# Newton steps of the norm with an operand in PSUM, and a softmax that starts its row minimum at the sink, in an encoder trunk on Trainium2

## The chip, the cores and the metric

The kernel runs on one core of one Trainium2 chip. The metric is the device time of one execution in microseconds (us); a version is described by the median of several executions. A core has five engines that run their own instruction streams and wait for each other by semaphores: TensorE (PE, the matrix engine, whose results land in the PSUM memory), VectorE (DVE), ScalarE (ACT), GpSimd (POOL), and SyncE (SP), which here issues nearly all DMAs. All other data of the kernel lie in the on-chip memory SBUF.

## The reference

Two token sequences, a prompt of 512 tokens and a sample of 1024, go through two layers with the same weights (model width 1024). What matters of one layer:

```python
hn = rmsnorm(h, ln1[i])                      # h * rsqrt(mean(h*h) + EPS) * gain
q, k, v, ga, uf, gf, mga, mgf = split(hn @ w_in[i])
a = band_attention(rope(q), rope(k), v, sink[i]) * silu(ga)
f = fourier_mix(uf, w_fmix[i]) * silu(gf)
h = h + (sigmoid(mga) * (a @ w_ao[i]) + sigmoid(mgf) * (f @ w_fo[i])) @ w_out[i]
h = h + (p[i] @ w_pe[i]) * sigmoid(rmsnorm(h, ln_pg[i]) @ w_pg[i])
```

and, inside the attention (8 query heads, 2 key heads, head width 64, a band of 128 tokens to each side, one sink number `sk` per head):

```python
m = maximum(max(s, axis=-1), sk)             # s = q k^T / 8, masked by -1e30
e = exp(s - m)
pr = e / (sum(e, axis=-1) + exp(sk - m))
```

A last rmsnorm gives the output.

## The kernel before

**Tiling.** Tokens are cut into three chunks of 512 columns: chunk 0 is the prompt, chunks 1 and 2 (called the pair) are the sample. Features lie on the 128 partitions, so that h of one chunk is 8 tiles of 128x512. All products are fp32 emulated by three matmuls: `hi_lo` splits an operand into a rounded high part (an ACT cast, L86) and the rest (a subtraction on DVE or POOL, L87), and `mm3` issues high by high, high by low and low by high (L98, L99, L100).

**Stages of a layer.** `project_prompt` computes the 34 column tiles of the input projection of the prompt, with three other streams woven in by `run`: making the normed pair, the prompt's attention, and the prompt's Fourier branch. `project_pair` does the projection of both sample chunks by a scheme with seven half products (L231 the matmuls, L238 to L260 the sums of them), with the pair's attention woven in. Then `merge` of the prompt, with the sample's Fourier branch beside it, and `merge` of the pair follow: branch projections, output projection, a norm, the gate projection, the residual update. The kernel is traced under a scheduler that takes the program order as priorities and sets each engine's final order from its own model of times and from free buffers. A different list of instructions in one place can so come out in another order on every engine nearby.

**The norm.** `Norm.add` sums squares of the 8 tiles. `Norm.stats` (L302 to L315) contracts them over partitions by four matmuls with a column of 1/1024 (L305) into columns 0 to 3 of a PSUM bank of the tag misc, 128 tokens on the partitions and 4 groups of tokens in the columns. L307 adds EPS, giving `v`; L309 and L310 make the first guess of 1/sqrt(v) by integer operations on the bits; three Newton steps of three operations each follow (L312 a product r * -0.5 * r, L313 a product with v, L314 the new r). All these are 128x4 operations on DVE; all but L307 read and write small SBUF tiles of the tag tiny. `Norm.scale` (L317 to L323) then turns r into a row form by four PE transposes into another misc bank (L320), and a DVE copy brings that to SBUF (L322). There are 15 such norms in a run. PE takes its instructions in order, so while L320 waits for the last L314, every matmul behind L320 waits too.

**The softmax.** A unit is 128 queries with one key head, thus 4 query heads; there are 8 units for the prompt and 16 for the sample per layer, 48 in all, with 192 heads. A unit's window W is 384 keys, at the two ends of a sequence 256. `scores(u)` (L658 to L689) does per head: two matmuls into a PSUM bank sc (L670, 2 banks), a custom DVE reduction (L675) that adds the mask, writes the masked scores to SBUF and the row maximum to `mx`, a DVE operation that makes the bias min(-0.125 mx, -sink) (L678), and the exponential on ACT with its row sum (L680). Then, once per unit, a DVE addition (L683), an exponential of the sink terms on ACT (L684), a DVE addition to the sum (L685), a DVE reciprocal (L686), and four ACT operations that scale the probabilities (L688). `values(u)` (L691 on) transposes the probabilities on PE (L707) into misc banks, splits them (L86 on ACT, L87 on DVE), and multiplies them with the values (L712) into the bank o. In the prompt, the program gives `scores(u)` ahead of `values(u-1)`; in the pair, `scores(u)` and `values(u)` follow each other with four slots of the projection between.

**Who else uses DVE and POOL.** The subtractions L87 go to DVE for activations and partly to POOL, above all for weights (386 of 128x512 from act tiles, and 72 from scr tiles, on POOL). The activation functions of the projection are finished on DVE (L427) after an ACT tanh (L426).

Of the kernel before, what the change touches and what calls it, by code (L numbers as in the profile page):

```python
# [18 lines left out]
P = 128  # L19
# [20 lines left out]
def trunk(ctx: ExitStack, tc: tile.TileContext, x, p, w_in, w_af, w_out, w_pe, w_pg, w_fm,  # L40
# [20 lines left out]
    def big(shape, dt=F32):  # L61
        return sbt(shape, dt, "act")
# [226 lines left out]
    class Norm:  # L289
# [12 lines left out]
        def stats(self):  # L302
            st = pst("misc")
            for j in range(4):
                PE.matmul(st[:, j : j + 1], self.acc[:, j * P : (j + 1) * P], mean_sb, start=True, stop=True)  # L305
            v, r, z = (sbt([P, 4], F32, "tiny") for _ in range(3))
            V.tensor_scalar(v, st[:, 0:4], EPS, None, op0=ALU.add)  # L307

            V.tensor_scalar(r.bitcast(I32), v.bitcast(I32), 1, None, op0=ALU.arith_shift_right)  # L309
            V.tensor_scalar(r.bitcast(I32), r.bitcast(I32), -1.0, float(0x5F3759DF), op0=ALU.mult, op1=ALU.add)  # L310
            for _ in range(3):
                V.scalar_tensor_tensor(z, r, -0.5, r, op0=ALU.mult, op1=ALU.mult)  # L312
                V.tensor_tensor(z, z, v, op=ALU.mult)  # L313
                V.scalar_tensor_tensor(r, z, 1.5, r, op0=ALU.add, op1=ALU.mult)  # L314
            self.r = r  # L315
# [316 lines left out]
    def attention(l, chunks, slim):  # L632
# [25 lines left out]
        def scores(u):  # L658
# [5 lines left out]
            mx, nmx, rs, es, rd = (sbt([P, 4], F32, "stat") for _ in range(5))  # L664
            probs = []
            for i in range(4):
# [4 lines left out]
                if i % 2 == 0:  # L671
                    t = big([P, 2, W])
                pr, e = t[:, i % 2, :], slice(i, i + 1)
                probs.append(pr)
                V.tensor_tensor_reduce(out=pr, in0=sc[:, :W], in1=msk, scale=1.0, scalar=-3.0e38,  # L675
                                       op0=ALU.add, op1=ALU.max, accum_out=mx[:, e])

                V.scalar_tensor_tensor(nmx[:, e], mx[:, e], -0.125, nsink_sb[:, l, head : head + 1],  # L678
                                       op0=ALU.mult, op1=ALU.min)
                S.activation(pr, pr, AF.Exp, bias=nmx[:, e], scale=0.125, accum_out=rs[:, e])  # L680
                if i % 2:
                    yield
            V.tensor_tensor(es, sink_sb[:, l, 4 * kv : 4 * kv + 4], nmx, op=ALU.add)  # L683
            S.activation(es, es, AF.Exp)  # L684
            V.tensor_tensor(rd, rs, es, op=ALU.add)  # L685
            V.reciprocal(rd, rd)  # L686
            for i, pr in enumerate(probs):
                S.activation(pr, pr, AF.Copy, scale=rd[:, i : i + 1])  # L688
# [419 lines left out]
```

## Time and profile before

| what | value |
|---|---|
| time, median of 3 runs | 2336.91 us (2334.51 to 2337.52) |
| profiled execution, its own time | 2336.8 us |
| its span in the trace | 2334.6 us |
| PE busy | 2211.7 us, 95% |
| DVE busy | 1424.6 us, 61% |
| POOL busy | 1113.4 us, 48% |
| ACT busy | 1088.9 us, 47% |
| mean granted TensorE clock | 0.98 |

The profile is of one execution. In its views, a row of the timeline gives the start and the duration in us, the engine, the source line, the operation, the tiles (out<-in), the shape, and how many instructions the row holds; in brackets stands how long the engine sat idle before it and what it waited for. A row of the groups gives after the bar the busy time in us and the mean duration in ns, and after the second bar the idle time before these instructions and what ended it. The view of one line gives min, median and max duration in ns, the first and last start, and the shapes. The view of waits gives, for PE, how long each line waited for which other line, in all, how many times, and the longest. A view of windows gives for stretches of time how long each engine was busy, with the number of instructions, and the granted clock of PE.

### The profile page before, as it was taken

The numbers are of one execution on the slowest core, as the hardware profiler recorded it, in microseconds if no ns is written. First come the engines' busy times: TensorE is split into PE (matmuls) and PEld (weight loads), VectorE is DVE, ScalarE is ACT, GpSimd is POOL, SyncE is SP. The second block draws the span as 40 slices with busy tenths as digits, with TensorE's granted clock in tenths as the row PEclk, the third lists the DMA queues.
The fourth block names the chain that finished last, engine by engine and source line by source line (L and its number), as shares of the span: only waits on it lengthen the run. The fifth ranks groups of instructions, "written<-read, shape, count | busy, mean of one in ns | idle before, by whom it ended". The sixth has DMA issues, their size and how long they took to land. (4 is left out here: it accounts for less than half of the span.)

```text
span 2334.6 us, 30544 instructions
## 1 busy us (share of the span) xinstructions
PE 2211.7 (95%) x10176; PEld 1812.2 (78%) x10176; DVE 1424.6 (61%) x2563; ACT 1088.9 (47%) x2292; POOL 1113.4 (48%) x827
## 2 busy tenths in 40 slices
PE   8899999999998989999999999899999999999986
PEld 6677777888877877888887787788787788788875
DVE  5866645677566775252767653657766666744376
ACT  5467433466664444223424853336666544422331
POOL 1313446444446863344514355644444568554471
PEclk9899999999999999999999999999999999999998
DMA  7565435445437464731445554453444655553232
GB/s 280 187 198 177 164 119 178 147 140 165 131 130 269 153 237 163 249 117 47 140 166 185 153 177 168 149 171 125 148 154 132 218 198 186 198 194 117 87 113 95
DMA packets 240542, 380.73 MB, mean 163 GB/s; under 512 B 21121, under 2 KB 95489, under 8 KB 240385
## 3 DMA queue, kind: packets, MB, share of 16 engines
q1 hardware_dynamic: 233472, 366.19, 46.6%
q10 hardware_dynamic: 6912, 12.59, 1.5%
q8 instruction: 81, 1.33, 0.2%
q14 instruction: 77, 0.62, 0.1%
HBM read 270.17 MB, written 108.53 MB: 162 GB/s over the span
## 5 line engine op out<-in xcount | busy, mean ns | idle before, releaser
L87 POOL TENSOR_TENSOR act<-act,act 128x512 fp32r<-128x512 f32 x386 | 547.2, 1437 | 463.4 <-ACT act L86 403.8
L231 PE MATMUL mm<-act,act 128*128 128x512 f32 x2856 | 700.4, 395 | 27.6 <-DVE act L87 11.7
L231 PEld LDWEIGHTS mm<-act,act 128*128 128x128 f32 x2856 | 531.1, 189 | 147.2 <-ACT act L86 18.0
L98 PE MATMUL mm<-act,act 128*128 128x512 f32 x1408 | 563.1, 400 | 29.6 <-ACT act L86 28.5
L100 PE MATMUL mm<-act,act 128*128 128x512 f32 x1408 | 559.3, 399 | 13.2 <-POOL act L87 13.2
L99 PE MATMUL mm<-act,act 128*128 128x512 f32 x1408 | 557.8, 396 | 0.0
L86 ACT CAST act<-act 128x512 fp32r<-128x512 f32 x574 | 330.1, 619 | 223.0 <-DMA act<-in_w_af 53.2
L98 PEld LDWEIGHTS mm<-act,act 128*128 128x128 f32 x1408 | 269.8, 192 | 88.6 <-ACT act L86 35.0
L100 PEld LDWEIGHTS mm<-act,act 128*128 128x128 f32 x1408 | 269.3, 191 | 78.2 <-POOL act L87 23.4
L99 PEld LDWEIGHTS mm<-act,act 128*128 128x128 f32 x1408 | 269.7, 192 | 54.0
L87 DVE TENSOR_TENSOR act<-scr,act 128x512 fp32r<-128x512 f32 x188 | 180.7, 979 | 102.8 <-ACT act L86 101.6
L86 ACT CAST act<-scr 128x512 fp32r<-128x512 f32 (+1 forms) x260 | 152.6, 614 | 170.8 <-DVE scr L382 79.0
L87 POOL TENSOR_TENSOR act<-scr,act 128x512 fp32r<-128x512 f32 (+1 forms) x72 | 100.1, 1392 | 207.6 <-ACT act L86 141.1
L87 DVE TENSOR_TENSOR act<-act,act 128x512 fp32r<-128x512 f32 x188 | 172.2, 944 | 35.7 <-ACT act L86 34.7
L300 POOL TENSOR_TENSOR scr<-scr,scr 128x512 f32<-128x512 f32 x67 | 94.5, 1411 | 173.5 <-ACT scr L299 164.1
L299 ACT ACTIVATE scr<-act 128x512 f32<-128x512 f32 x105 | 65.3, 632 | 236.8 <-DVE act L540 148.1
L680 ACT ACTIVATE act<-act,stat 128x384 f32<-128x384 f32 (+1 forms) x192 | 111.0, 580 | 68.9 <-DVE stat L678 68.5
L87 DVE TENSOR_TENSOR act<-misc,act 128x512 fp32r<-128x512 f32 x132 | 88.5, 687 | 76.8 <-ACT act L86 76.3
L86 ACT CAST act<-misc 128x512 fp32r<-128x512 f32 x132 | 73.7, 586 | 96.1 <-PE misc L707 93.6
L675 DVE CUSTOM_DVE_ANT_0 act<-sc,mask_sb 128x384 f32<-128x384 f32 (+1 forms) x192 | 92.4, 508 | 41.8 <-PE sc L670 36.7
L100 PE MATMUL sc<-act,act 128*128 128x512 f32 (+1 forms) x292 | 111.8, 383 | 1.1 <-DVE act L87 1.1
L98 PE MATMUL sc<-act,act 128*128 128x512 f32 (+1 forms) x292 | 111.5, 383 | 0.0
(209 smaller groups left out, 3019.3 us busy)
## 6 DMA issues: line engine op xcount, KB each, us to landing
act<-in_w_in SPq DMA_DIRECT2D x136, 256.0 KB, 4.3
act<-in_w_in SPq DMA_DIRECT2D x68, 512.0 KB, 4.7
gt<-scr SPq DMA_DIRECT2D x96, 256.0 KB, 2.3
scr<-gt SPq DMA_DIRECT2D x96, 256.0 KB, 5.3
act<-in_w_pg SPq DMA_DIRECT2D x80, 256.0 KB, 3.7
act<-in_w_af SPq DMA_DIRECT2D x64, 256.0 KB, 4.8
act<-in_w_out SPq DMA_DIRECT2D x64, 256.0 KB, 4.9
pl<-scr ACTq DMA_DIRECT2D x48, 256.0 KB, 2.5
```

The source lines that it names most:

```text
L86: S.copy(hi, src)
L87: lo_eng.tensor_tensor(lo, src, f(hi), op=ALU.subtract)
L98: PE.matmul(out, wh, xh, start=i == 0, stop=False)
L99: PE.matmul(out, wh, xl, start=False, stop=False)
L100: PE.matmul(out, wl, xh, start=False, stop=i == n - 1)
L231: PE.matmul(bank, w, v, start=first and k == 0 and n == 0, stop=k == 3 and n == 2, skip_group_check=True)
L299: S.activation(sq, h, AF.Square)
L300: eng.tensor_tensor(self.acc, self.acc, sq, op=ALU.add)
L675: V.tensor_tensor_reduce(out=pr, in0=sc[:, :W], in1=msk, scale=1.0, scalar=-3.0e38, op0=ALU.add, op1=ALU.max, accum_out=mx[:, e])
L680: S.activation(pr, pr, AF.Exp, bias=nmx[:, e], scale=0.125, accum_out=rs[:, e])
```

## The change

In `Norm.stats`, v, y (the shifted bits) and z get columns 4 to 15 of the PSUM bank that holds the sums, in place of SBUF tiles; r stays in an SBUF tile of the tag tiny. The first two operations of a Newton step change places: z = v * r, then z = z * -0.5 * r. There are 12 DVE operations as before; each now has one operand in PSUM and at most one tensor in SBUF. The misc bank of the sums is held until the last Newton step, where it was free after L307 before.

In `scores`, the reduction scales by -0.125 and takes the minimum, and begins at the negated sink (a per-partition scalar read through a pointer to SBUF, where it was the constant -3e38), so that it yields the bias itself. L678 is gone. The masked scores are now scaled when they are written, and the exponential has scale -1. The tile of two heads has one more column, into which a new ACT copy of 128x2 (L676 of the changed kernel, one per two heads) writes the negated sink; the exponential runs over W+1 columns, so its row sum includes the sink's term, and L683, L684 and L685 are gone. The reciprocal takes the row sum directly, and the normalisation runs over W columns. Per unit, 6 DVE operations and one on ACT go, and two on ACT come.

In the changed kernel the lines stand a little lower: L320 becomes L322, L670 becomes L672, L675 becomes L680, L680 becomes L683, L427 becomes L429; the reciprocal stays L686 and the normalisation L688.

```diff
@@ -303,14 +303,16 @@
             st = pst("misc")
             for j in range(4):
                 PE.matmul(st[:, j : j + 1], self.acc[:, j * P : (j + 1) * P], mean_sb, start=True, stop=True)
-            v, r, z = (sbt([P, 4], F32, "tiny") for _ in range(3))
+
+            v, y, z = (st[:, 4 * j : 4 * j + 4] for j in range(1, 4))
+            r = sbt([P, 4], F32, "tiny")
             V.tensor_scalar(v, st[:, 0:4], EPS, None, op0=ALU.add)
 
-            V.tensor_scalar(r.bitcast(I32), v.bitcast(I32), 1, None, op0=ALU.arith_shift_right)
-            V.tensor_scalar(r.bitcast(I32), r.bitcast(I32), -1.0, float(0x5F3759DF), op0=ALU.mult, op1=ALU.add)
+            V.tensor_scalar(y.bitcast(I32), v.bitcast(I32), 1, None, op0=ALU.arith_shift_right)
+            V.tensor_scalar(r.bitcast(I32), y.bitcast(I32), -1.0, float(0x5F3759DF), op0=ALU.mult, op1=ALU.add)
             for _ in range(3):
-                V.scalar_tensor_tensor(z, r, -0.5, r, op0=ALU.mult, op1=ALU.mult)
-                V.tensor_tensor(z, z, v, op=ALU.mult)
+                V.tensor_tensor(z, v, r, op=ALU.mult)
+                V.scalar_tensor_tensor(z, z, -0.5, r, op0=ALU.mult, op1=ALU.mult)
                 V.scalar_tensor_tensor(r, z, 1.5, r, op0=ALU.add, op1=ALU.mult)
             self.r = r
 
@@ -661,7 +663,7 @@
             W = (k1 - k0) * P
             msk = mask_sb[:, (k0 - qb + 1) * P : (k1 - qb + 1) * P]
             q, kw = blocks[c, b][kv]["q"], blocks[c, b][kv]["kw"]
-            mx, nmx, rs, es, rd = (sbt([P, 4], F32, "stat") for _ in range(5))
+            nmx, rs, rd = (sbt([P, 4], F32, "stat") for _ in range(3))
             probs = []
             for i in range(4):
                 head = 4 * kv + i
@@ -669,23 +671,21 @@
                 for j in range(2):
                     PE.matmul(sc[:, :W], q[:, i, :], kw[:, j, :], start=j == 0, stop=j == 1)
                 if i % 2 == 0:
-                    t = big([P, 2, W])
+
+                    t = big([P, 2, W + 1])
+                    S.copy(t[:, :, W], nsink_sb[:, l, head : head + 2])
                 pr, e = t[:, i % 2, :], slice(i, i + 1)
                 probs.append(pr)
-                V.tensor_tensor_reduce(out=pr, in0=sc[:, :W], in1=msk, scale=1.0, scalar=-3.0e38,
-                                       op0=ALU.add, op1=ALU.max, accum_out=mx[:, e])
-
-                V.scalar_tensor_tensor(nmx[:, e], mx[:, e], -0.125, nsink_sb[:, l, head : head + 1],
-                                       op0=ALU.mult, op1=ALU.min)
-                S.activation(pr, pr, AF.Exp, bias=nmx[:, e], scale=0.125, accum_out=rs[:, e])
+
+                V.tensor_tensor_reduce(out=pr[:, :W], in0=sc[:, :W], in1=msk, scale=-0.125,
+                                       scalar=nsink_sb[:, l, head : head + 1],
+                                       op0=ALU.add, op1=ALU.min, accum_out=nmx[:, e])
+                S.activation(pr, pr, AF.Exp, bias=nmx[:, e], scale=-1.0, accum_out=rs[:, e])
                 if i % 2:
                     yield
-            V.tensor_tensor(es, sink_sb[:, l, 4 * kv : 4 * kv + 4], nmx, op=ALU.add)
-            S.activation(es, es, AF.Exp)
-            V.tensor_tensor(rd, rs, es, op=ALU.add)
-            V.reciprocal(rd, rd)
+            V.reciprocal(rd, rs)
             for i, pr in enumerate(probs):
-                S.activation(pr, pr, AF.Copy, scale=rd[:, i : i + 1])
+                S.activation(pr[:, :W], pr[:, :W], AF.Copy, scale=rd[:, i : i + 1])
             blocks[c, b][kv]["probs"] = probs
 
         def values(u):
```

The order of the instructions also changes, in the attention stages only; the rows that follow were printed without times. In the prompt of the first layer, PE reaches its first scores as follows in the kernel before (L98 to L100 are projection matmuls, `sc` the score banks, `misc` the banks of the transposes, and the numbers behind the names count tiles):

```order
L670 MATMUL sc_1167<-act_1125,scr_1123 128x256 x2
L670 MATMUL sc_1174<-act_1125,scr_1123 128x256 x2
L98 MATMUL mm_1287<-act_346,act_1154 128x512
L99 MATMUL mm_1287<-act_346,act_1154 128x512
L670 MATMUL sc_1199<-act_1131,scr_1129 128x256 x2
L670 MATMUL sc_1206<-act_1131,scr_1129 128x256 x2
L100 MATMUL mm_1287<-act_346,act_1154 128x512
L98 MATMUL mm_1287<-act_360,act_1154 128x512
```

Projection matmuls stand between the scores of the first unit (sc_1167, sc_1174) and those of the second (sc_1199, sc_1206) here, and 22 more follow ahead of the next scores. After the change PE has, from the third head of the first unit on (sc_1158; the second unit's scores begin at sc_1184, the third's stand further on):

```order
L672 MATMUL sc_1158<-act_1119,scr_1117 128x256 x2
L672 MATMUL sc_1165<-act_1119,scr_1117 128x256 x2
L672 MATMUL sc_1184<-act_1125,scr_1123 128x256 x2
L672 MATMUL sc_1191<-act_1125,scr_1123 128x256 x2
L672 MATMUL sc_1202<-act_1125,scr_1123 128x256 x2
L707 MATMUL misc_1223<-ident_sb,act_1133 128x128
L707 MATMUL misc_1238<-ident_sb,act_1133 128x128
L672 MATMUL sc_1209<-act_1125,scr_1123 128x256 x2
L707 MATMUL misc_1223<-ident_sb,act_1133 128x128
L707 MATMUL misc_1238<-ident_sb,act_1133 128x128
```

The scores of the first units now follow each other with the transposes of the first unit (L707) between them, and the projection matmuls that stood between the units' scores and the transposes stand ahead of all of it.

On DVE, at the same place in the prompt of the first layer, before the change (the second unit's reductions are those with act_1202; ISA rows are the reduction and the read of its accumulator):

```order
L87 TENSOR_TENSOR act_1157<-act_1076,act_1157 128x512
L678 SCALAR_TENSOR_TENSOR stat_1134<-stat_1133,nsink_sb 128x1 x2
L683 TENSOR_TENSOR stat_1136<-sink_sb,stat_1134 128x4
L685 TENSOR_TENSOR stat_1137<-stat_1135,stat_1136 128x4
L675 ISA act_1202,stat_1194<-sc_1199,mask_sb 128x256
L675 ISA stat_1194 128x1
L675 ISA act_1202,stat_1194<-sc_1206,mask_sb 128x256
L675 ISA stat_1194 128x1
L686 RECIPROCAL stat_1137<-stat_1137 128x4
```

Here the reciprocal comes last, since it waits for L685 and that for the exponential of L684. After the change DVE has at that place (the second unit's are those with act_1187):

```order
L680 ISA act_1161,stat_1127<-sc_1158,mask_sb,nsink_sb 128x256
L680 ISA stat_1127 128x1
L680 ISA act_1161,stat_1127<-sc_1165,mask_sb,nsink_sb 128x256
L680 ISA stat_1127 128x1
L686 RECIPROCAL stat_1129<-stat_1128 128x4
L680 ISA act_1187,stat_1181<-sc_1184,mask_sb,nsink_sb 128x256
L680 ISA stat_1181 128x1
L680 ISA act_1187,stat_1181<-sc_1191,mask_sb,nsink_sb 128x256
L680 ISA stat_1181 128x1
```

The reciprocal of the first unit moved from behind the first two reductions of the second unit to ahead of them, and four small operations between went.

## The prediction

> **What bounds the kernel now.** I read the page first, then PE's waits, then the timeline at PE's longest waits. The page gives each engine's busy time:
>
> ```profile
> span 2334.6 us, 30544 instructions
> ...
> PE 2211.7 (95%) x10176; PEld 1812.2 (78%) x10176; DVE 1424.6 (61%) x2563; ACT 1088.9 (47%) x2292; POOL 1113.4 (48%) x827
> ```
>
> PE is busy for 2211.7 of 2334.6 us, and the change takes no matmul away. So it can only gain where PE waits (2334.6 - 2211.7 = 123 us in all) or runs at a lower clock. A shorter DVE or ACT is worth nothing by itself. PE's waits, by the line that ends them (total, times, longest):
>
> ```profile
> PE mm L98 <- ACT act L86: 28.5, 12, 7.6
> PE misc L320 <- DVE tiny L314: 13.0, 4, 6.2
> PE mm L231 <- DVE act L87: 11.7, 8, 2.2
> PE mm L231 <- DVE stat L685: 2.5, 2, 1.2
> PE sc L670 <- DVE stat L675: 1.9, 4, 0.9
> PE misc L707 <- ACT act L688: 0.9, 5, 0.2
> ```
>
> The change touches the second row in full (norm to transposes: 13.0 us in four waits) and the other DVE rows in part. The largest wait of the norm lies in the last merge, at 2231 us; DVE, POOL and PE there:
>
> ```profile
> 2217.49 0.16 DVE L307 TENSOR_SCALAR tiny<-misc 128x4 f32<-128x4 f32 x1
> 2229.76 1.19 DVE L314 SCALAR_TENSOR_TENSOR tiny<-tiny,tiny 128x4 f32<-128x4 f32 x1
> 2215.10 23.26 POOL L87 TENSOR_TENSOR act<-act,act 128x512 fp32r<-128x512 f32 x18
> 2224.49 0.39 PE L100 MATMUL sc<-act,act 128*128 128x512 f32 x1
> 2231.09 1.09 PE L320 MATMUL misc<-ident_sb,tiny 128*128 128x128 f32 x4 [6.21 <-DVE tiny L314]
> 2231.83 0.78 PE L98 MATMUL sc<-act,act 128*128 128x512 f32 x1
> 2236.24 0.46 PE L99 MATMUL sc<-act,act 128*128 128x512 f32 x1
> ```
>
> While POOL runs its subtractions back to back, twelve 128x4 operations take from 2217.49 to 2230.95, the last of them 1.19 us. The first, which reads PSUM, takes 0.16. At the end of the run, with POOL idle, the whole row of twelve goes through unhindered:
>
> ```profile
> 2320.42 0.16 DVE L307 TENSOR_SCALAR tiny<-misc 128x4 f32<-128x4 f32 x1 [2.02 <-PE misc L305]
> 2322.90 1.09 PE L320 MATMUL misc<-ident_sb,tiny 128*128 128x128 f32 x4 [2.52 <-DVE tiny L314]
> ```
>
> That is 2.48 us from L307 to the transposes, against 13.60 at 2217. The same holds of each operation over the run (min, median, max in ns), and of a larger one that comes with and without a PSUM operand:
>
> ```profile
> L307 DVE TENSOR_SCALAR tiny<-misc x15: 146/163/163, 28.8 to 2320.4; 128x4 f32<-128x4 f32 x15
> L313 DVE TENSOR_TENSOR tiny<-tiny,tiny x45: 152/161/1224, 29.6 to 2322.4; 128x4 f32<-128x4 f32 x45
> L427 DVE SCALAR_TENSOR_TENSOR scr<-scr,mm x24: 673/685/690, 106.2 to 1653.8; 128x512 f32<-128x512 f32 x24
> L427 DVE SCALAR_TENSOR_TENSOR scr<-scr,scr x24: 684/693/1819, 396.1 to 1664.4; 128x512 f32<-128x512 f32 x24
> ```
>
> The operations of one kind have the same minimum; only those whose tensors all lie in SBUF ever reach 1.2 us (or 0.7 + 1.1). They seem to wait for the POOL instruction that is under way. The reductions L675, which read PSUM, don't.
>
> **Part one, the Newton steps.** The change gives each of the twelve operations a PSUM operand and at most one SBUF tensor. No DVE operation writes PSUM in the trace, so its price is bounded: from below by 0.15 us (L307, L313), from above by the locked 1.22. I take 0.16, the row with PSUM as source, since only the side of the operand differs. A Newton chain then takes 2.5 us everywhere.
>
> At 2217.49 that ends at about 2220.0, and PE gets to L320 at 2224.88 (end of the last L100). The wait of 6.21 us goes with 4.9 us to spare. Something goes with it: after the wait the matmuls start 0.43 us apart in place of 0.23 until 2236.2 (ten between 2231.83 and 2236.24, spacing 0.44), so half clock costs about 10 x 0.21 = 2.1 us. Of the time from there to the last norm this window tells (PE's busy time comes first, the clock after POOL's):
>
> ```profile
> 2217.00:2311.00 94.00, 87.79 (x393) 72.59 (x392) 67.24 (x94) 31.42 (x56) 51.33 (x37) 0.96 0.32 107
> ```
>
> 94.00 - 87.79 is 6.21, so PE waits for nothing else, and the shift of 8.3 us reaches the end. The second place is in the merge of the prompt, first layer:
>
> ```profile
> 855.63 0.15 DVE L307 TENSOR_SCALAR tiny<-misc 128x4 f32<-128x4 f32 x1
> 860.10 0.39 PE L100 MATMUL mm<-act,act 128*128 128x512 f32 x1
> 864.63 1.11 PE L320 MATMUL misc<-ident_sb,tiny 128*128 128x128 f32 x4 [4.14 <-DVE tiny L314]
> 867.25 0.58 PE L99 MATMUL mm<-act,act 128*128 128x512 f32 x1
> ```
>
> Here 855.63 + 2.5, and a subtraction of 0.7 between, is 858.8, before PE's 860.49: 4.14 us go, with 1.7 to spare, and five matmuls at half clock give 5 x 0.21 = 1.1 more. Next PE waits for casts on ACT which stand behind the tanh of the products that PE has just made, so they come earlier too. Of the four waits, the one at the end (2.52) stays, since it is the unhindered chain, and 13.0 - 6.21 - 4.14 - 2.52 leaves 0.1 for the fourth. The other eleven norms have matmuls over them. Sum: 6.21 + 2.1 + 4.14 + 1.1 = **-13.5 us**. If a PSUM write costs more, the spare times hide up to 0.14 us an operation (1.7 / 12); only the last chain shows it, 12 times.
>
> [...]
>
> In the merge stages PE and DVE keep their order. The misc bank of the sums is now held for 2.5 us more, 15 times; the attention's transposes and the Fourier branch take banks of that tag too. No wait for a bank stands among PE's waits, so I put it at nothing; at most it is 2.5 us where a norm stands beside that work.
>
> **Part two, less softmax on DVE.** These groups go (busy us, mean ns), and the copies come at the price of the last row:
>
> ```profile
> L678 DVE SCALAR_TENSOR_TENSOR stat<-stat,nsink_sb 128x1 f32<-128x1 f32 x192 | 82.5, 446 | 1.2
> L683 DVE TENSOR_TENSOR stat<-sink_sb,stat 128x4 f32<-128x4 f32 x48 | 23.6, 491 | 1.4
> L685 DVE TENSOR_TENSOR stat<-stat,stat 128x4 f32<-128x4 f32 x48 | 18.6, 389 | 17.4 <-ACT stat L684 16.9
> L773 ACT CAST tiny<-scr x8: 188/191/206, 213.3 to 1393.0; 128x2 fp32r<-128x2 f32 x8
> ```
>
> DVE loses 82.5 + 23.6 + 18.6 = 124.7 us. What a start value through a pointer adds to the reduction no row tells; it lies between nothing and the 0.16 us of a small operation, 192 times (31 us of DVE at most, beside PE). ACT gets 96 x 0.19 = 18 us and one more column, and loses 48 exponentials of four columns. Off PE's path all this is worth nothing. In the pair's stages it ends waits of this kind:
>
> ```profile
> 526.09 1.23 DVE L678 SCALAR_TENSOR_TENSOR stat<-stat,nsink_sb 128x1 f32<-128x1 f32 x1
> 527.98 0.51 PE L231 MATMUL mm<-act,act 128*128 128x512 f32 x1 [1.18 <-DVE act L87]
> ```
>
> The subtraction that PE needs stood behind a locked L678. There are two such places per layer: this one (1.18), and one behind L685 (the row of 2.5 us in two waits). Together that is 2 x 1.2 x 2 = 4.8 us. The order in the pair also changes (below, third rival), so I give 2 us back: **-2.8**.
>
> **Part three, the new order at the prompt's attention.** As the order rows above show, the scores of units 0 to 2 now come nearly without projection matmuls between, and DVE's reciprocal of unit 0 stands ahead of unit 1's reductions. It waits for four exponentials on ACT; behind it wait the reductions, and with two sc banks PE's scores. Before, the 22 matmuls covered that. The rows for ACT, PE, and the window of 16 us:
>
> ```profile
> 134.81 0.51 ACT L680 ACTIVATE act<-act,stat 128x256 f32<-128x256 f32 x1 [0.89 <-DVE stat L678]
> 138.78 1.71 ACT L688 ACTIVATE act<-act,stat 128x256 f32<-128x256 f32 x4 [1.35 <-DVE stat L678]
> 142.93 0.56 ACT L86 CAST act<-misc 128x512 fp32r<-128x512 f32 x1
> 132.00:148.00 16.00, 13.49 (x65) 9.97 (x64) 9.56 (x40) 10.87 (x32) 2.57 (x2) 1.00 0.94 307
> 1275.67 0.74 PE L670 MATMUL sc<-act,scr 128*128 128x256 f32 x4 [1.68 <-DMA scr<-q]
> ```
>
> A unit of 256 keys holds ACT for 4 x 0.51 + 1.71 + 2 x 0.56 + 2 x 0.19 = 5.2 us. Two of these and half of a third unit's exponentials (1.4), with 0.7 for the first scores and reduction, are 12.5 us; in that stretch PE has some 21 projection matmuls at 0.23 and about 40 small ones, an estimate of 9.8 us. PE idles 2.7 us; with each hand-over walked through one after another it is 4.6. Before, the window of 16 us has 2.5 idle. I take the upper end, **+2.5 per layer, +5.0**, because hand-overs between four engines rarely overlap fully. Since the scores come 16 matmuls later, the wait of 1.68 us for q goes, with the half clock behind it (about 1.6) and 0.3 in the first layer: **-3.6**. The clock after the new waits is unsure. This trace has half clock after short gaps:
>
> ```profile
> 219.10:222.50 3.40, 1.79 (x8) 1.16 (x8) 2.22 (x5) 2.77 (x10) 2.46 (x5) 1.00 0.56 213
> 222.50:229.30 6.80, 6.75 (x18) 5.53 (x19) 4.99 (x14) 3.97 (x11) 4.21 (x4) 0.50 0.98 293
> ```
>
> PE was busy for 1.79 of 3.40 us, no single gap longer than about a microsecond, and ran at a clock of 0.50 for the next 6.8 us (3.4 us of work lost). I count half of one such window, **+1.7**. [...]
>
> **Sum**, against the profiled execution's own 2336.8 us (the median is 2336.91, the same): -13.5 - 2.8 + 5.0 - 3.6 + 1.7 = -13.2, so **2323.6 us**. Its own range, from the bounds above, is 2318 to 2331.
>
> **The rivals.** *First, attention gains too:* the prompt's onset idles at its lower end (+0.5 in each layer), no clock falls, and the pair loses its four waits: -13.5 - 4.8 + 1.0 - 3.6 = -20.9, 2316. For it: DVE is freed of 125 us. Against it: the denser order. *Second, the prompt eats the gain:* two windows of half clock per layer, 4 x 3.4 = 13.6 in place of the 1.7, so 2335.5, no difference. For it: the two windows above. Against it: the onset before idled for 2.5 of 16 us and kept a clock of 1.00. *Third, slower:* in the pair's stages the second half of a unit's scores now stands about 24 matmuls ahead of its transposes, where it was about 36, so PE has 24 x 0.23 = 5.5 us of cover in place of 8.2 for reduction, exponential, reciprocal, normalisation (some 4 us of work when ACT is free). If ACT's queue makes that 0.41 us too short in each of the 32 pair units, the gain is gone; slower begins at 0.56 us, and at 0.75 us the time is 2347.6. Against it: transposes waited for L688 for only 0.9 us in all. *Fourth, the change doesn't do what it says:* writing PSUM doesn't keep DVE from waiting for POOL, the chains stay as they are, and with the rest 2337 comes out.
>
> **How the numbers follow.** Forecast 0.53, first rival 0.18, second 0.16, third 0.08, fourth 0.05. A measurement of this kernel tells about 0.2% (4.7 us) from no change. Faster: the forecast but for 0.01, all of the first rival, 0.03 of the second: 0.73. Slower: the third, 0.02 of the second, 0.01 of the fourth: 0.11. The same: the rest, 0.16. The range of 8 in 10 goes from 2312 (below the first rival's 2316 by what the cover of the pair might add) to 2338 (above the second and fourth); the third and the edges are left out.
>
> **What would show it.** Right: all Newton operations at 0.15 to 0.23 us beside a busy POOL, no wait of L322 but the last (about 2.5 us), a clock of 1.00 after 2220 and 860; the waits for DVE L87 of 1.18 gone. Waits of scores and transposes for ACT and DVE at the prompt's start, 5 to 9 us over both layers. Wrong: operations of 1.2 us in the Newton chain (fourth), rows of clock 0.50 in the prompt (second), waits of the transposes L707 for L688 in each unit of the pair (third).

## The result, and the profile after

The changed kernel takes 2298.98 us (median of 4 runs, 2296.27 to 2300.48), the kernel before 2336.12 on the same chip: a ratio of 0.984 with a 95% interval of 0.9823 to 0.9857, so 33 to 41 us less. The forecast was 13.2 less, with a range that ended at 2312. The direction was right; the size was not. The page of the changed kernel:

```profile
span 2294.5 us, 30367 instructions
...
PE 2192.3 (96%) x10176; PEld 1808.6 (79%) x10176; DVE 1306.0 (57%) x2275; ACT 1087.9 (47%) x2340; POOL 1116.1 (49%) x827
```

The span is 40.1 us shorter. PE's idle time fell from 122.9 to 102.2 us, by 20.7. PE's busy time fell too, by 19.4 us, with the same 10176 matmuls. So half of the gain is not in any "idle" column. Two things hide in a busy PE. A matmul that starts after a wait has a longer row (0.50 us in place of 0.39, with its successor 0.33 later in place of 0.23), and matmuls at half clock start about 0.43 us apart in place of 0.23.

To see where the time went, I cut both traces at the same matmuls (the 380th, the first and last L231 of each layer, and the 870th ahead of the second layer's L231). Rows of the windows, with the length, PE's busy time and, after POOL's, the granted clock; of the kernel before the first layer's prompt stage and pair stage, the second layer's pair, and the last merge:

```profile
109.37:315.59 206.22, 195.48 (x911) 159.31 (x910) 123.01 (x307) 115.30 (x285) 64.18 (x54) 0.95 0.51 168
315.59:727.73 412.14, 395.92 (x1828) 323.33 (x1827) 268.74 (x496) 224.49 (x483) 201.74 (x148) 1.00 0.47 157
1455.18:1867.74 412.56, 396.20 (x1828) 323.25 (x1827) 268.71 (x496) 224.58 (x483) 201.74 (x148) 1.00 0.48 159
1867.74:2323.57 455.83, 432.44 (x1990) 357.46 (x1988) 272.28 (x401) 161.88 (x302) 255.03 (x186) 0.98 0.43 147
```

The same of the changed kernel:

```profile
108.33:308.10 199.77, 189.08 (x911) 156.76 (x910) 116.94 (x259) 115.61 (x293) 63.39 (x54) 0.97 0.52 173
308.10:710.62 402.52, 392.51 (x1829) 323.26 (x1828) 231.35 (x400) 223.79 (x499) 201.91 (x148) 1.00 0.48 161
1430.63:1832.91 402.28, 392.47 (x1828) 323.32 (x1827) 231.41 (x400) 223.90 (x499) 201.86 (x148) 1.00 0.49 162
1832.91:2283.47 450.56, 431.96 (x1989) 357.76 (x1988) 258.91 (x401) 161.79 (x302) 259.19 (x186) 0.98 0.44 150
```

With the stages not shown (start 101.81 to 101.00, first merge 534.32 to 531.37, second layer's prompt 193.13 to 188.64) the gains are:

| part | forecast | in the two traces |
|---|---|---|
| both merges (Newton) | -13.5 | -2.95 and -5.27 = -8.2 |
| both pair stages | -2.8 | -9.62 and -10.28 = -19.9 |
| both prompt stages | +3.1 | -6.45 and -4.49 = -10.9 |
| start | 0 | -0.8 |
| sum | -13.2 | -39.9 |

In the pair stages 6.2 and 6.6 us of idle time and 3.4 and 3.7 us of busy time went. PE's waits in the second layer's pair stage (total, times, longest), before:

```profile
PE mm L231 <- DVE act L87: 5.9, 4, 2.1
PE mm L231 <- ACT act L86: 4.2, 3, 2.5
PE o L712 <- ACT act L86: 2.3, 4, 0.6
PE mm L231 <- POOL act L87: 1.9, 1, 1.9
PE mm L231 <- DVE stat L685: 1.2, 1, 1.2
```

and after:

```profile
PE mm L231 <- DVE act L87: 4.3, 3, 2.0
PE mm L231 <- ACT act L86: 3.6, 2, 2.5
PE mm L231 <- DVE scr L242: 1.0, 1, 1.0
PE o L712 <- ACT act L86: 0.6, 1, 0.6
```

The two waits that I had priced are gone (1.18 us, a part of the first row, and 1.23 behind L685), 2.4 us together. The other 4 us of idle time were waits that I had not priced: three of the four for the cast ahead of L712, and part of those at the stage's end, for POOL among them. No line of the list names L678.

In the merges the chain of twelve does what was forecast, also while POOL works (the first and last operation at the place that took 13.6 us, and the transposes, which no longer wait):

```profile
2182.84 0.17 DVE L309 TENSOR_SCALAR misc<-misc 128x4 f32<-128x4 f32 x1
2185.07 0.16 DVE L316 SCALAR_TENSOR_TENSOR tiny<-misc,tiny 128x4 f32<-128x4 f32 x1
2190.07 0.60 PE L322 MATMUL misc<-ident_sb,tiny 128*128 128x128 f32 x4
```

But new waits stand a little later, one in each merge:

```profile
859.27 0.63 PE L98 MATMUL mm<-act,act 128*128 128x512 f32 x1 [3.80 <-ACT act L86]
2233.06 1.14 PE L305 MATMUL misc<-mean_sb,scr 128*128 128x1 f32 x9 [1.57 <-DVE scr L300]
```

### The profile page after: what moved, and what is told of

The parts are those of the page before. It is cut to its first block, busy times and chain, and to the rows that moved or that the text cites. A ratio compares the mean times of both kernels' runs of the same rounds, so it can differ in the third digit from the quotient of the medians.

```text
span 2294.5 us, 30367 instructions
## 1 busy us (share of the span) xinstructions
PE 2192.3 (96%) x10176; PEld 1808.6 (79%) x10176; DVE 1306.0 (57%) x2275; ACT 1087.9 (47%) x2340; POOL 1116.1 (49%) x827
## 5 line engine op out<-in xcount | busy, mean ns | idle before, releaser
L231 PE MATMUL mm<-act,act 128*128 128x512 f32 x2856 | 700.4, 394 | 18.7 <-DVE act L87 8.5
L231 PEld LDWEIGHTS mm<-act,act 128*128 128x128 f32 x2856 | 531.0, 189 | 133.3 <-ACT act L86 16.3
L98 PE MATMUL mm<-act,act 128*128 128x512 f32 x1408 | 561.6, 399 | 32.5 <-ACT act L86 30.3
L100 PE MATMUL mm<-act,act 128*128 128x512 f32 x1408 | 557.9, 398 | 11.7 <-POOL act L87 11.7
L98 PEld LDWEIGHTS mm<-act,act 128*128 128x128 f32 x1408 | 269.1, 191 | 89.8 <-ACT act L86 34.6
L100 PEld LDWEIGHTS mm<-act,act 128*128 128x128 f32 x1408 | 268.7, 191 | 73.9 <-POOL act L87 19.7
L87 DVE TENSOR_TENSOR act<-act,act 128x512 fp32r<-128x512 f32 x188 | 183.6, 1005 | 35.3 <-ACT act L86 34.6
L683 ACT ACTIVATE act<-act,stat 128x385 f32<-128x385 f32 (+1 forms) x192 | 110.7, 579 | 47.1 <-DVE stat L680 46.9
L680 DVE CUSTOM_DVE_ANT_0 act<-sc,mask_sb,nsink_sb 128x384 f32<-128x384 f32 (+1 forms) x192 | 104.2, 569 | 48.1 <-PE sc L672 29.1
L100 PE MATMUL sc<-act,act 128*128 128x512 f32 (+1 forms) x292 | 111.1, 381 | 0.9 <-DVE act L87 0.9
L98 PE MATMUL sc<-act,act 128*128 128x512 f32 (+1 forms) x292 | 111.1, 381 | 0.0
```

Of the source, the lines that this page charges most:

```text
L87: lo_eng.tensor_tensor(lo, src, f(hi), op=ALU.subtract)
L98: PE.matmul(out, wh, xh, start=i == 0, stop=False)
L100: PE.matmul(out, wl, xh, start=False, stop=i == n - 1)
L231: PE.matmul(bank, w, v, start=first and k == 0 and n == 0, stop=k == 3 and n == 2, skip_group_check=True)
L680: V.tensor_tensor_reduce(out=pr[:, :W], in0=sc[:, :W], in1=msk, scale=-0.125, scalar=nsink_sb[:, l, head : head + 1], op0=ALU.add, op1=ALU ...
L683: S.activation(pr, pr, AF.Exp, bias=nmx[:, e], scale=-1.0, accum_out=rs[:, e])
```

## The experiments

Times are medians, each beside the kernel before on the same chip; the ratio is to that.

**1 and 2: the two parts apart.** The Newton hunk of the diff alone, and the softmax hunks alone.

```diff
# run 1: only Norm.stats
-            v, r, z = (sbt([P, 4], F32, "tiny") for _ in range(3))
+            v, y, z = (st[:, 4 * j : 4 * j + 4] for j in range(1, 4))
+            r = sbt([P, 4], F32, "tiny")
...
# run 2: only scores()
-                V.scalar_tensor_tensor(nmx[:, e], mx[:, e], -0.125, nsink_sb[:, l, head : head + 1],
-                                       op0=ALU.mult, op1=ALU.min)
...
```

> The kernel before with the Newton part of the change alone. Theory (the Newton part gives little, since the subtractions queued behind it on DVE now wait for POOL in its place, and attention gives most): about 2329 us, 7 us less than before, 2 of it in the merge of the first layer's prompt and 5 in the last merge. Rival (the prediction's own sum): 13.5 us less, 2322.6. Both: pair and prompt stages as before.

> The softmax part alone, Newton steps as before. Theory: about 30 us less than before, 2306, some 10 in each layer's pair stage and 5 to 7 in each layer's prompt stage. Rival (the prediction): parts two and three of the sum, +0.3, 2336. A second rival (the two parts need each other): the sum of both runs' gains falls short of the 37 us of the whole change by over 8 us.

Measured: Newton alone 2326.54, ratio 0.9957 (0.9945 to 0.9968), 10 us less; softmax alone 2307.33, ratio 0.9874 (0.986 to 0.9889), 29 us less. The first lies between both expectations, the second is the theory's. Together they make 40, against 37 for both: the parts add up and do not need each other. In run 1 the pair stages are as before (412.3 and 412.2 us), and the two merges are 4.3 and 5.2 us shorter. So the largest term that failed is the attention's.

**3 and 4: the softmax part divided.** Run 3 has the minimum that begins at the sink, and keeps L683 to L685; run 4 has the column, and keeps L678.

```diff
# run 3
-                V.tensor_tensor_reduce(out=pr, in0=sc[:, :W], in1=msk, scale=1.0, scalar=-3.0e38,
-                                       op0=ALU.add, op1=ALU.max, accum_out=mx[:, e])
-                V.scalar_tensor_tensor(nmx[:, e], mx[:, e], -0.125, nsink_sb[:, l, head : head + 1],
-                                       op0=ALU.mult, op1=ALU.min)
+                V.tensor_tensor_reduce(out=pr, in0=sc[:, :W], in1=msk, scale=-0.125,
+                                       scalar=nsink_sb[:, l, head : head + 1],
+                                       op0=ALU.add, op1=ALU.min, accum_out=nmx[:, e])
...
# run 4
+                    S.activation(t[:, :, W], nsink_sb[:, l, head : head + 2], AF.Copy, scale=-8.0)
...
-            V.tensor_tensor(es, sink_sb[:, l, 4 * kv : 4 * kv + 4], nmx, op=ALU.add)
-            S.activation(es, es, AF.Exp)
-            V.tensor_tensor(rd, rs, es, op=ALU.add)
-            V.reciprocal(rd, rd)
+            V.reciprocal(rd, rs)
...
```

> From the softmax part only the reduction that begins at the sink and gives the bias itself; L678 is gone, the sink's additions and exponential (L683 to L685) stay. Theory (what counts is the chain from the scores to the transposes, of which L678 is the part that each head waits for): more than half of the softmax part's gain, 18 us less than before, 2318. Rival (the chain at a unit's end counts, with its way from DVE to ACT and back): 5 us less, 2331.

> From the softmax part only the column for the sink; L683, L684 and L685 are gone, the maximum and L678 stay. Theory (L678 is the larger part): 10 us less than before, 2326. Rival (the chain at a unit's end counts): 20 us or more less, 2316.

Measured: 2322.15, ratio 0.9938 (0.9926 to 0.9951), 15 us less; and 2328.16, ratio 0.9961 (0.9947 to 0.9975), 9 us less. L678 is probably the larger part, as the theory had it (the two intervals overlap a little), though smaller than its 18, and the two make 24 of the 29 us.

**5, 6 and 7: DVE's time, the chain, and the wait for POOL.** Each adds one 128x1 operation per head to the changed kernel. In run 5 nobody reads its result; in run 6 the exponential does; in run 7 it does too, but the form is one that has a single SBUF tensor and a pointer.

```diff
# run 5
...
+                V.scalar_tensor_tensor(un[:, e], nmx[:, e], -0.125, nsink_sb[:, l, head : head + 1],
+                                       op0=ALU.mult, op1=ALU.min)
# run 6
...
+                V.scalar_tensor_tensor(un[:, e], nmx[:, e], 1.0, nsink_sb[:, l, head : head + 1],
+                                       op0=ALU.mult, op1=ALU.min)
-                S.activation(pr, pr, AF.Exp, bias=nmx[:, e], scale=-1.0, accum_out=rs[:, e])
+                S.activation(pr, pr, AF.Exp, bias=un[:, e], scale=-1.0, accum_out=rs[:, e])
# run 7: as run 6, with
+                V.tensor_scalar(un[:, e], nmx[:, e], 1.0, nsink_sb[:, l, head : head + 1],
+                                op0=ALU.mult, op1=ALU.min)
```

> The changed kernel with one more 128x1 operation of two SBUF operands on DVE per head, right behind the reduction, whose result nobody reads: DVE gets L678's work back, the chain from the scores to the exponential doesn't. Theory (the chain of a unit counts, not DVE's time): as the changed kernel, 2299 to 2303 us. Rival (DVE's time and its waits for POOL count, wherever they stand): some 14 us go back, as the run with the minimum alone gained, 2313.

> The same operation with a result that the exponential waits for (the minimum with the negated sink, which leaves the value as it is): DVE's work as in the run before, but in the chain. Theory (chain): 14 us go back, 2313. Rival (DVE's time): the same time as the run before, whatever that is.

> The operation in the chain again, but in a form with one SBUF tensor and the sink through a pointer, which should not wait for POOL (0.13 to 0.2 us each time in place of up to 1.3). Theory (in the chain, the waits for POOL make most of L678's price): 3 to 5 us go back, 2303. Rival (the extra hand-over itself, or the order that the scheduler makes for it, is the price): 14 us go back, 2313.

Measured, with the changed kernel at 2301.78 beside them (run 8, ratio 0.9845, 0.9827 to 0.9863): run 5 has 2305.0 (0.9866, 0.985 to 0.9882), run 6 2325.34 (0.9954, 0.994 to 0.9968), run 7 2318.87 (0.9923, 0.991 to 0.9936). The groups of the added operation, of run 5:

```profile
L683 DVE SCALAR_TENSOR_TENSOR stat<-stat,nsink_sb 128x1 f32<-128x1 f32 x192 | 84.5, 456 | 1.4
```

of run 6:

```profile
L683 DVE SCALAR_TENSOR_TENSOR stat<-stat,nsink_sb 128x1 f32<-128x1 f32 x192 | 82.1, 443 | 1.6
```

and of run 7, in the view of the line (min, median and max in ns):

```profile
L683 DVE TENSOR_SCALAR stat<-stat,nsink_sb x192: 195/207/218, 139.4 to 1814.8; 128x1 f32<-128x1 f32 x192
```

Runs 5 and 6 give DVE the same 82 to 85 us of work and the same waits for POOL. Beside the chain it costs 3 us, which the intervals hardly tell from nothing; in the chain it costs 24, more than the 14 that the theory had. Run 7's operation never waits for POOL and still costs 17. That is near its rival (14), and the theory (3 to 5) was wrong. So about 17 of the 24 come with the place between the reduction and the exponential, and some 6 with the waits for POOL there (each time has an interval of about 3 us); that DVE has less to do is worth little, as the prediction said. The rival of run 7 names the hand-over and the new order together, and runs 6 and 7 don't separate these: matched by line and tile names, run 5 has 1823 of the 1828 matmuls of a pair stage in the changed kernel's order, run 6 1717 and run 7 1721. Runs 10 and 11 bear on that. The second layer's pair stage in run 5,

```profile
1436.48:1839.95 403.47, 393.38 (x1829) 323.32 (x1827) 256.56 (x464) 223.69 (x499) 201.38 (x148) 1.00 0.48 160
```

in run 6,

```profile
1445.23:1857.42 412.19, 396.26 (x1828) 324.48 (x1827) 260.91 (x464) 224.53 (x499) 201.91 (x148) 0.99 0.48 160
```

and in run 7:

```profile
1447.34:1856.13 408.79, 394.38 (x1828) 323.38 (x1827) 242.83 (x464) 223.56 (x499) 203.39 (x148) 1.00 0.48 161
```

402.28 in the changed kernel, 403.47, 412.19, 408.79: run 6 has the length of the kernel before (412.56) again, although L683 to L685 are gone in it.

**8: the changed kernel again, for the clock.**

> The changed kernel once more, for its time beside these runs and for a second trace of the TensorE clock. Theory (half clock follows when PE streams for less than about 0.4 of a window of 3.41 us on a grid that each execution places anew): the same waits at the same places within 0.1 us, but half clock in partly other places; 2299 us. Rival (half clock follows from the waits themselves): the same places of half clock as in the first trace.

The waits stand at the same places: 1.10 and 1.95 us at the start of the first pair stage, 1.10 and 1.94 in the first trace. The clock does not. In the first trace (length, PE's busy time, then the others, the clock after POOL's):

```profile
313.40:316.80 3.40, 2.09 (x8) 0.89 (x6) 3.00 (x4) 3.40 (x8) 1.97 (x2) 1.00 0.50 202
316.80:320.20 3.40, 1.68 (x7) 1.42 (x8) 3.37 (x2) 0.55 (x2) 3.40 (x3) 1.00 0.00 0
320.20:323.60 3.40, 3.40 (x16) 2.82 (x16) 0.90 (x2) 0.00 (x0) 2.36 (x2) 1.00 0.02 5
```

In the second:

```profile
314.50:317.90 3.40, 2.30 (x10) 1.13 (x8) 2.60 (x3) 3.40 (x8) 1.57 (x2) 1.00 0.64 263
317.90:321.30 3.40, 1.45 (x7) 1.07 (x7) 3.40 (x3) 0.95 (x2) 3.40 (x3) 1.00 0.00 0
321.30:324.70 3.40, 3.40 (x10) 2.62 (x9) 1.05 (x2) 0.00 (x0) 2.72 (x2) 0.50 0.00 0
```

All changes of the clock in a trace lie on a grid of 3.41 us, which lies elsewhere in each execution (from the span's start at 0.65 us and every 3.41 us after that in the kernel before, at 2.75 in the first trace). The same two waits share out to 2.09 and 1.68 us of busy PE in the one and leave 1.45 in a single window in the other, and only the latter is followed by half clock. PE's busy time also holds the longer rows after waits. Counted instead as 0.227 us of work for each 512 columns, the window of 1.68 us holds 1.53 (0.45 of the window) and that of 1.45 holds 1.18 (0.35). The window of the kernel before at 219.1 us, with 1.79 us busy and half clock behind it, holds 0.96 (0.28). Up to the last matmul, half clock adds up to 62 us in the first trace and 80 in the second. The theory holds: 0.45 of a window kept the full clock, 0.35 and 0.28 did not.

**9: L678 in the form that doesn't wait, in the kernel before.**

```diff
-                V.scalar_tensor_tensor(nmx[:, e], mx[:, e], -0.125, nsink_sb[:, l, head : head + 1],
-                                       op0=ALU.mult, op1=ALU.min)
+                V.tensor_scalar(nmx[:, e], mx[:, e], -0.125, nsink_sb[:, l, head : head + 1],
+                                op0=ALU.mult, op1=ALU.min)
```

> The kernel before with L678 in the form with one SBUF tensor and the sink through a pointer (it took 195 to 218 ns in the run before and never waited for POOL); everything else, the number of operations too, stays, and so does PE's order in the pair's stages nearly. Theory (of L678's price some quarter is its waiting for POOL, the rest its place in the chain): 5 to 8 us less than before, 2330. Rival (the waiting for POOL is all of it): 18 us less, 2318. Second rival (it is nothing, since the scheduler's order decides): within 3 us of before.

Measured: 2325.58, ratio 0.996 (0.9947 to 0.9973), 9 us less, with every L678 between 183 and 215 ns. The theory had 5 to 8. The waiting for POOL is part of the price, not all of it and not nothing; its pair stages are 408.91 and 409.25 us long, a third of the way to the changed kernel's. How large that part is depends on the kernel. With the time lost to half clock taken out (half of its length), the pair stages of run 9 are 3.2 and 3.4 us shorter than before, and those of run 3, without L678, 5.5 and 6.8: here the waiting is about half of L678's price. Counted the same way, run 6's pair stages are 8.7 and 8.2 us longer than the changed kernel's and run 7's 5.5 and 6.5, so there it is a fifth to two fifths.

**10 and 11: with PE's order nearly held.**

```diff
-    with tile.TileContext(nc, schedule_with_timeline_sim=True) as tc:
+    with tile.TileContext(nc, schedule_with_timeline_sim=False) as tc:
```

> The kernel before, with the scheduler's own model of times switched off, so that its order follows the program and the buffers. No theory has its time; it is the base of the next run.

> The changed kernel in that same way. In the pair's stages PE's order now hardly differs between the two (1779 of 1827 matmuls in common, against 1621 with the model on). Theory (the shorter chain gains by itself): the pair's stages are 7 to 10 us each shorter than in the run before, the whole 25 to 35 us. Rival (the new order that the scheduler's model makes is the gain): the pair's stages within 3 us of the run before, the whole 10 to 13 us less, by the Newton part.

Measured: 2371.55 (ratio 1.0158, 1.0145 to 1.0171) and 2332.48 (0.9993, 0.9984 to 1.0002), so the change gains 39 us here, where it gained 37 before (the theory had 25 to 35). The second layer's pair stage of run 10,

```profile
1461.06:1880.93 419.87, 403.35 (x1829) 325.96 (x1827) 238.96 (x495) 224.18 (x482) 197.44 (x148) 0.98 0.46 150
```

and of run 11:

```profile
1443.36:1846.87 403.51, 393.67 (x1828) 322.89 (x1827) 218.96 (x399) 224.91 (x498) 198.63 (x148) 1.00 0.47 156
```

It is 16 us shorter, some 7 of them by the clock (17.1 us of half clock in run 10, 3.4 in run 11); 9 to 10 remain, as in the kernels with the scheduler's model on. The first layer's is 12.0 us shorter, 1.7 of them by the clock. The new order is not what gains in the pair stages.

**12: the same cure on one more chain.** The gate's two DVE operations get an operand in PSUM.

```diff
-            S.activation(a, a, AF.Tanh, scale=0.5)
-            V.scalar_tensor_tensor(a, a, 1.0, pl, op0=ALU.add, op1=ALU.mult)
+            S.activation(out, a, AF.Tanh, scale=0.5)
+            V.scalar_tensor_tensor(out, out, 1.0, pl, op0=ALU.add, op1=ALU.mult)
             h = hs[c][m // 2][:, m % 2, :]
-            V.scalar_tensor_tensor(h, a, 0.5, h, op0=ALU.mult, op1=ALU.add)
+            V.scalar_tensor_tensor(h, out, 0.5, h, op0=ALU.mult, op1=ALU.add)
```

> The changed kernel with the gate's tanh written back into the PSUM bank of its product, so that the two DVE operations behind it (the product with the embedding and the sum with h, 24 and 24 in the last merge at 1.12 and 1.14 us) have one SBUF tensor each and no longer wait for POOL. Theory (what counts is a chain that PE waits for; in the merges PE has enough matmuls over this one but at two places): 1 to 4 us less than the changed kernel, 2296. Rival (the banks that are held longer stop PE, or the locks only move on to the subtractions behind): no gain or a loss up to 5 us.

Measured: 2290.21, ratio 0.9812 (0.9799 to 0.9825), some 7 us below the changed kernel by the ratios (0.984 and 0.9845, whose intervals just meet and just miss this one), more than the theory's 1 to 4. This is the fastest version. The product with the embedding in the changed kernel,

```profile
L560 DVE SCALAR_TENSOR_TENSOR scr<-scr,scr x48: 677/693/1853, 850.7 to 2275.5; 128x512 f32<-128x512 f32 x48
```

and in this run, where it is of one length (32 of the 48; the others, on other banks, take 0.70 us too):

```profile
L560 DVE SCALAR_TENSOR_TENSOR mm<-mm,scr x32: 684/699/700, 853.9 to 2271.7; 128x512 f32<-128x512 f32 x32
```

The two new waits of the merges answer to it: 3.80 us at 859 became 0.84 and 1.25, and 1.57 at 2233 is gone. Of the gain in the last merge (450.6 to 442.7 us) some 5 us are clock, 17.7 us of half clock against 7.2. The theory had the right place; how much of the surplus over its 4 us is the clock of these executions stays open.

## Why the prediction was wrong

**What bounds the kernel.** That only PE's waits and clock can gain was right, and DVE's time by itself was rightly put at nothing (run 5: 3 us). Not right was to count PE's idle time as all that a wait costs. In the first pair stage 6.2 us of idle time and 3.4 us of busy time went, with the same half clock in both (3.4 us) and 11 idle gaps of PE in place of 25: some 0.24 us per gap on top of the idle time, which was in no term of the sum.

**Part one, Newton** (-13.5). What it counted on held: the operations that read or write PSUM take 0.15 to 0.18 us, all 180 of them in the changed kernel, beside a busy POOL too, and both waits went. Run 1 measured 10 us in all, its merges 9.5, where the sum had 13.5. The step that failed is "Next PE waits for casts on ACT which stand behind the tanh of the products that PE has just made, so they come earlier too", and "the shift of 8.3 us reaches the end". POOL's row of subtractions is not over when the Newton steps no longer wait for it; the subtractions that stand behind them on DVE now collide with it. In the first merge, the operations behind the chain before:

```profile
864.52 1.29 DVE L87 TENSOR_TENSOR act<-act,act 128x512 fp32r<-128x512 f32 x2
...
866.46 0.68 DVE L87 TENSOR_TENSOR act<-act,act 128x512 fp32r<-128x512 f32 x1
...
868.25 1.29 DVE L87 TENSOR_TENSOR act<-scr,act 128x512 fp32r<-128x512 f32 x2
```

and after:

```profile
842.02 3.01 DVE L87 TENSOR_TENSOR act<-act,act 128x512 fp32r<-128x512 f32 x2
...
845.56 1.18 DVE L87 TENSOR_TENSOR act<-act,act 128x512 fp32r<-128x512 f32 x1
...
848.36 2.38 DVE L87 TENSOR_TENSOR act<-scr,act 128x512 fp32r<-128x512 f32 x2
```

Before, POOL's row of subtractions had ended at 863.57 us, ahead of these (of the chain's steps in SBUF the six up to then took 1.07 to 1.25 us, the five after it 0.16 to 0.17); now it lasts from 836.59 to 847.89, through most of them. The tanh and the casts behind them therefore come only some 3 us earlier against the chain's start (20.0 us behind it at 858.60, where it was 22.9), and the wait of 1.60 us at the stage's end became 3.80. So PE's idle time fell by 1.8 us in the first merge and 4.8 in the last, not by 4.14 and 6.21. The terms for the clock hardly came either (1.1 and 2.1): the first merge has 6.8 us of half clock before and after, now behind the new wait, and the last 18.9 and 17.7, a gain of 0.6. Run 1 has the new waits too (3.80, and 1.66 in the last merge), and run 12, which takes waits for POOL from the same DVE queue, loses most of them.

**Part two, the pair** (-2.8). This is the step that failed most: "There are two such places per layer", priced by the waits behind L678 and L685 alone, with 2 us given back for the order. Both waits went, 2.4 us in each layer, but the stages became 9.6 and 10.3 us shorter; the other waits, the busy time of PE that goes with waits, together 7 to 8 us per layer, had no term. Nothing had to be given back for the order. An operation in the chain of each head delays the exponential, the reciprocal, the transposes and the casts of that unit, and PE meets the delay under other names: L712 behind the cast (in the second layer's pair 2.3 us before and 0.6 after), L231 behind a subtraction (5.9 and 4.3), the end of the stage. That the chain is what counts is shown: DVE's work off the chain costs 3 us and in it 24 (runs 5 and 6), and with PE's order nearly held (1779 of 1827 matmuls) the softmax part as a whole still gains 9 to 10 us per pair stage (runs 10 and 11). By which of the steps between the exponential and L231 the delay reaches PE was not followed one by one.

**Part three, the prompt** (+5.0 - 3.6 + 1.7). All three terms failed. The first was also reckoned loosely: 4.6 us of idle time against 2.5 before makes +2.1 per layer, not +2.5. The waits at the onset after the change:

```profile
136.12 0.74 PE L672 MATMUL sc<-act,scr 128*128 128x256 f32 x4 [1.19 <-DMA scr<-q]
139.30 0.91 PE L672 MATMUL sc<-act,scr 128*128 128x256 f32 x4 [0.35 <-DVE stat L680]
141.08 0.50 PE L672 MATMUL sc<-act,scr 128*128 128x256 f32 x2 [0.87 <-DVE stat L680]
144.88 0.50 PE L712 MATMUL o<-act,act 128*128 128x512 f32 x1 [1.43 <-ACT act L86]
```

Scores and transposes wait for 0.35 + 0.87 + 1.43 = 2.65 us: the lower end of the walk (2.7), where I took the upper (4.6) on an estimate of how hand-overs overlap that no trace had shown. The wait for q did not go but grew, to 1.19 and in the second layer 2.25 (1.80 and 2.71 in the trace of run 8): on SP two loads of weights and a load of keys and one of values now stand between the second unit's keys and the loads of q. These start 20.3 us into the first layer's stage, where it was 17.9, and land in 7.5 us in place of 5.6 (medians). I had looked at PE's order and not at SP's. SP's rows before,

```profile
126.80 0.46 SPq L651 DMA_DIRECT2D act<-k  x1
127.31 2.07 SPq L649 DMA_DIRECT2D scr<-q  x3
```

and after:

```profile
125.73 0.46 SPq L653 DMA_DIRECT2D act<-k  x1
126.30 0.88 SPq L158 DMA_DIRECT2D act<-in_w_in  x2
127.27 0.38 SPq L653 DMA_DIRECT2D act<-k  x1
127.75 0.83 SPq L657 DMA_DIRECT2D act<-v  x1
128.63 2.57 SPq L651 DMA_DIRECT2D scr<-q  x3
```

The clock went the other way: half clock in the two prompt stages fell from 21.0 and 13.7 us to 10.5 and 6.8, worth 8.7 us of PE's work, most of the 10.9 gained there. By run 8 such amounts depend on where the grid falls in an execution (62 and 80 us of half clock in two traces of one kernel), so one pair of traces can't put them down to the change; the medians' 37 us against the traces' 40 may be of that kind. Six traces say more. The two prompt stages together take 399.4 and 397.6 us with the old softmax (the kernel before, run 1) and 388.4, 388.8, 390.9 and 391.7 with the new one (the changed kernel, runs 2, 8 and 12). So some 8 us of the gain recur, 4 of them with the time lost to half clock taken out. Runs 10 and 11 have 384.0 and 382.9, a gain of only 1.1 us, but of 6 with that time taken out (10.2 us of half clock in run 10, 20.4 in run 11). So 4 to 6 us are the change's own, where the sum had +3.1, and the clock adds to this or takes from it.

**The chances.** "Faster" had 0.73. The first rival ("attention gains too", 2316) named the right direction with a quarter of attention's gain (7.4 of 30.8 us): it too counted only four waits of the pair.

## What to carry to other kernels

Price an operation by its place: here one that each unit's chain runs through cost far more than the waits that carry its line's name, since the delay shows under the names of what comes after it (17 to 24 us), and one off the chain cost almost nothing (3 us), even with the same waits for another engine. Where a wait for POOL is taken from one DVE operation, look at what is queued behind it, because POOL's work is still there (here the next two subtractions took 3.01 us in place of 1.29). And look at every queue whose order changes, SP's too, before a wait for a DMA is struck from the sum (here the one for q grew from 1.68 to 2.25 us).

## What the runs showed of the hardware

- TensorE's clock changed only at points 3.41 us apart, on a grid that differed from execution to execution. Counting 0.227 us of work per 512 columns, in the fourteen traces 203 windows at full clock were followed by half clock; PE had worked in each of them for at most 0.41 of the window, and no window below 0.33 was followed by full clock. In the kernel before and the changed one alone these are 13 and 11 windows, with at most 0.33 and 0.38; the lowest followed by full clock had 0.40 and 0.37. In the kernel before, two waits of 0.93 and 0.75 us at the two ends of one window (219.1), with short matmuls between (0.28 of the window), were followed by half clock.
- A DVE operation of 128x4 that reads and writes PSUM takes 0.155 to 0.178 us in the changed kernel; the whole Newton chain of the last norm has 2.57 us with PSUM operands and had 2.52 without, so PSUM operands are nearly free here.
- An operation of 128x1 with one SBUF tensor and a per-partition pointer never waited for POOL in run 9 (L678, 183 to 215 ns over 192 of them, where the form before reached 1311 ns), though all its operands lie in SBUF; it has the longer median (206 against 159 ns). A single SBUF tensor alone is not what spares an operation: in the kernel before, L309 and L310, of 128x4 with one SBUF tensor and constants, reached 1.07 and 1.22 us.
- The reduction that begins at a pointer takes 0.06 us more than the one before, which begins at a constant (mean 613 against 553 ns at 128x384). The change also gave it another scale and the minimum for the maximum; no run takes these apart.
